# A list scheduler that orders a two-block kernel's engine work: measured operation times in its cost table in place of estimates

## The chip, the cores and the metric

The kernel runs on one core of a Trainium2 chip. Times are device microseconds (us) of one execution of the whole program on that core. PE is the matrix engine, DVE the vector engine, ACT the scalar engine, POOL the GpSimd engine and SP the engine whose queue issues most DMAs. Each engine takes its own instructions strictly in the order in which the program emits them, and waits on semaphores for what other engines have to deliver.

## What is computed

The input is x, 1024 tokens of 1024 numbers in float32. Two blocks run one after the other, and the result of the second is the output:

```python
def first_block(x, mem, ...):
    h = rms_norm(x, norm_mix);  proj = h @ w_in
    # 8 query heads over 2 key/value heads, a window of 128, plus a gated spatial unit
    attn = sliding_window_attention(q, k, v, attn_sinks)
    sg = spatial_gating(u, g, sgu_norm, sgu_w, sgu_b)
    x = x + concat(rms_norm(attn), rms_norm(sg)) @ w_out
    x = x + memory_cross_attention(rms_norm(x, norm_cross), mem_n, ...)
    x = x + hierarchical_moe(rms_norm(x, norm_ffn), ...)     # 4 groups x 8 experts, top 2 of a group
...
def second_block(x, c, w_mod, b_mod, ...):
    shift1, scale1, gate1, shift2, scale2, gate2 = split(silu(c) @ w_mod + b_mod, 6)
    h = rms_norm_2(x, g_norm1) * (1 + scale1) + shift1
    x_lru, z_lru, q, k, v = split(h @ w_in)
    y_lru = (rg_lru(conv(x_lru), forwards) + rg_lru(conv(x_lru), backwards)) * gelu(z_lru)
    y_att = diff_attention(q, k, v, ...)                     # 4 heads: softmax 1 - lam * softmax 2
    x = x + gate1 * (concat(y_lru, y_att) @ w_out)
    h2 = rms_norm_2(x, g_norm2) * (1 + scale2) + shift2
    x = x + gate2 * expert_choice_ffn(h2, ...)               # 16 experts, each takes its top 128 tokens
```

An expert of the first block is `(silu(xe @ w1) * (xe @ w3)) @ w2` with 512 hidden numbers; one of the second has 1024.

## The kernel before

**Tiles.** The tokens are eight tiles of 128. Every large product is taken to more than one pass of precision: a weight chunk of 128x1024 numbers (512 KB) comes by DMA into `wraw` (L369), ACT copies it to `wh` (L384) in the matrix engine's rounded format, and DVE, or POOL where the schedule picks it, takes the rest `wl = wraw - wh` (L389). The activations are split alike when they are transposed (`xT_h` by ACT at L247, `xT_l` by DVE at L249). Each 128x512 step then is three matmuls, `wh` by the high part (L339), `wl` by the high part (L340), `wh` by the low part (L341), and a chunk has two such steps, six matmuls. Where columns of a weight are to be scaled by a gain, POOL does it in `wraw` first (L379).

**Stages**, by the trace: the first block's mixers to 690 us, its routing to 745, 32 experts (the "first expert loop") to about 1365, the second block's projections and recurrence to 1675, differential attention to 1859, output product and the expert choice to 2045, and 16 experts (the "second expert loop") to 2600.

**An expert** (`expert1` in the first loop) gathers its rows (`xe`, a POOL DMA, L1507), transposes them (`p_t`), makes `p_a` and `p_b` from four chunks of w1 and four of w3, multiplies `hid = silu(p_a) * p_b` on DVE (L1536), transposes that (`p_ht`, L269; the copies of it to SBUF are `hidT`, on ACT L247 and DVE L249), makes two `p_y` from four chunks of w2, scales them on ACT (`y`, L1550) and adds them into the output by an indirect DMA that POOL issues (L1559). The second block starts after the last of these.

**Differential attention** runs for each of 32 pairs of head and token tile: scores `p_sc` on PE (L2108, L2109), bias and maximum on DVE (L2115), exponentials on ACT (L2098), the two softmaxes combined into `s` on DVE (L2145) or on ACT and POOL (L2148, L2150), four transposes `p_wt` (L312) copied to `wT` by ACT (L315) or DVE (L317), the product `p_o` (L2159), a norm (its root on POOL, L2166), `o` on DVE (L2170) and a transpose `p_ot` (L2175).

**The expert choice** (`top_part`) finds each expert's 128 largest of 512 tokens in one half of the tokens, and a second part does the other half: 16 rounds on DVE of eight maxima (L2307), a replacement (L2310) and their indices (L2312). `p_top` (L2338) transposes the result.

**What sets the order.** No order is written out. Every piece of work is a Python generator that yields, ahead of the instructions it emits, `S.op(engine, cost)`, `S.get(class)` for a buffer, or `S.wait(event)`. `Sched.run` (L100 on) keeps a clock for each engine; of all pieces that may run it takes the one with the earliest start, and among equal starts the one with the better priority. The clock moves on by the cost given, and what depends on the result may start `HOP` later. Where a piece names two engines (`wl` on DVE or POOL, `wT` on ACT or DVE), the one that would end first by these clocks is taken. So the costs set the order of each engine's instructions, the choice of engine, and which loads are issued first; the chip then runs each engine's list at its own pace. Buffers are counted by class (48 slots in all are shared by weights and activations).

## Time and profile before

| | us |
| --- | --- |
| median of 3 runs (2614.12 to 2623.0) | 2618.95 |
| the profiled execution | 2611.75 |
| its span on the core | 2609.7 |
| PE busy in the span | 2396.9 (92%) |
| DVE busy | 1964.9 (75%) |
| ACT busy | 1573.1 (60%) |
| POOL busy | 484.5 (19%) |

The profiled execution is 7.2 us under the median of the runs, and 2.05 us of it lie outside the span. Busy times count instructions in flight. The matmuls of one product overlap in the profile: one is listed with about 0.39 us and the next begins 0.23 us after it. An engine's idle time is listed with the instruction that it waited for, and this is what the rows below show.

### The profile page before, as it was taken

The numbers are of one execution on the slowest core, as the hardware profiler recorded it, in microseconds if no ns is written. First come the engines' busy times: TensorE is split into PE (matmuls) and PEld (weight loads), VectorE is DVE, ScalarE is ACT, GpSimd is POOL, SyncE is SP. The second block draws the span as 40 slices with busy tenths as digits, with TensorE's granted clock in tenths as the row PEclk, the third lists the DMA queues.
The fourth block names the chain that finished last, engine by engine and source line by source line (L and its number), as shares of the span: only waits on it lengthen the run. The fifth ranks groups of instructions, "written<-read, shape, count | busy, mean of one in ns | idle before, by whom it ended". The sixth has DMA issues, their size and how long they took to land. (4 is left out here: it accounts for less than half of the span.)

```text
span 2609.7 us, 34986 instructions
## 1 busy us (share of the span) xinstructions
PE 2396.9 (92%) x11984; PEld 1973.6 (76%) x11984; DVE 1964.9 (75%) x3179; ACT 1573.1 (60%) x2414; POOL 484.5 (19%) x383
## 2 busy tenths in 40 slices
PE   7999999999889899999987999999892999999998
PEld 6888887888667777777765777788682788877786
DVE  6568558555788888888876547599649799899997
ACT  5357225442357778777774558587422777677775
POOL 1021011100321224111112201034533000110010
PEclk9999999999989999999998999999996999999999
DMA  4433465224579999999994212753326899999997
GB/s 155 150 114 102 166 243 213 60 82 167 187 256 310 320 316 312 356 338 345 347 304 127 72 60 75 196 143 107 126 97 229 283 362 359 375 372 378 375 375 254
DMA packets 314581, 600.70 MB, mean 230 GB/s; under 512 B 33097, under 2 KB 64397, under 8 KB 314401
## 3 DMA queue, kind: packets, MB, share of 16 engines
q1 hardware_dynamic: 299936, 562.74, 61.6%
q0 software_dynamic: 14464, 35.71, 5.5%
q8 instruction: 95, 1.56, 0.2%
q14 instruction: 86, 0.70, 0.1%
HBM read 554.25 MB, written 60.87 MB: 236 GB/s over the span
## 5 line engine op out<-in xcount | busy, mean ns | idle before, releaser
L389 DVE TENSOR_TENSOR wl<-wraw,wh 128x1024 fp32r<-128x1024 f32 x829 | 992.9, 1241 | 128.9 <-ACT wh L384 118.4
L384 ACT ACTIVATE wh<-wraw 128x1024 fp32r<-128x1024 f32 x852 | 846.1, 1051 | 89.3 <-DMA wraw<-in_w_ck_dram 34.4
L260 POOL TENSOR_TENSOR rs_r<-rs_v,mhalf 128x1 f32<-128x1 f32 (+2 forms) x111 | 103.6, 935 | 788.0 <-DVE rs_v L257 787.8
L340 PE MATMUL p_b<-wl,xT_h 128*128 128x512 f32 x512 | 203.0, 396 | 9.1 <-DVE wl L389 9.1
L340 PE MATMUL p_a<-wl,xT_h 128*128 128x512 f32 x512 | 204.1, 399 | 5.7 <-DVE wl L389 5.4
L339 PE MATMUL p_b<-wh,xT_h 128*128 128x512 f32 x512 | 205.4, 401 | 1.6 <-ACT wh L384 1.6
L339 PE MATMUL p_a<-wh,xT_h 128*128 128x512 f32 x512 | 206.3, 403 | 0.0
L341 PE MATMUL p_a<-wh,xT_l 128*128 128x512 f32 x512 | 201.3, 393 | 0.2 <-DVE xT_l L249 0.2
L341 PE MATMUL p_b<-wh,xT_l 128*128 128x512 f32 x512 | 200.7, 392 | 0.0
L339 PE MATMUL p_g<-wh,aT_h 128*128 128x512 f32 x384 | 157.4, 410 | 0.0
L341 PE MATMUL p_g<-wh,aT_l 128*128 128x512 f32 x384 | 150.9, 393 | 0.0
L340 PE MATMUL p_g<-wl,aT_h 128*128 128x512 f32 x384 | 150.8, 393 | 0.0
L1559 POOL DMA_INDIRECT x_d<-y,tok x32 | 59.7, 1864 | 347.2 <-ACT y L1550 327.7
L340 PEld LDWEIGHTS p_a<-wl,xT_h 128*128 128x128 f32 x512 | 97.1, 190 | 35.3 <-DVE wl L389 17.1
L340 PEld LDWEIGHTS p_b<-wl,xT_h 128*128 128x128 f32 x512 | 96.7, 189 | 35.5 <-DVE wl L389 16.9
L2399 POOL DMA_INDIRECT out_dram<-y,tok x16 | 38.0, 2372 | 451.2 <-DVE y L2389 346.3
L247 ACT ACTIVATE xT_h<-p_t 128x512 fp32r<-128x512 f32 x96 | 56.7, 595 | 97.7 <-PE p_t L269 97.1
L339 PEld LDWEIGHTS p_b<-wh,xT_h 128*128 128x128 f32 x512 | 96.7, 189 | 21.0 <-ACT wh L384 1.9
L341 PEld LDWEIGHTS p_a<-wh,xT_l 128*128 128x128 f32 x512 | 96.8, 189 | 20.2 <-DVE xT_l L249 0.6
L339 PEld LDWEIGHTS p_a<-wh,xT_h 128*128 128x128 f32 x512 | 97.2, 190 | 19.0
L341 PEld LDWEIGHTS p_b<-wh,xT_l 128*128 128x128 f32 x512 | 96.4, 188 | 19.6
L340 PE MATMUL p_y<-wl,hidT 128*128 128x512 f32 x256 | 103.9, 406 | 4.6 <-DVE wl L389 4.3
(500 smaller groups left out, 5801.1 us busy)
## 6 DMA issues: line engine op xcount, KB each, us to landing
wraw<-in_w_dram SPq DMA_DIRECT2D x768, 512.0 KB, 9.2
mraw<-in_w_mod_dram SPq DMA_DIRECT2D x48, 512.0 KB, 5.2
x<-x_d SPq DMA_DIRECT2D x32, 512.0 KB, 4.2
wraw<-in_w_in_dram SPq DMA_DIRECT2D x28, 512.0 KB, 7.9
wraw<-in_w_out_dram SPq DMA_DIRECT2D x16, 512.0 KB, 3.5
hd<-kT_d SPq DMA_DIRECT2D x32, 256.0 KB, 5.5
x<-in_x_dram SPq DMA_DIRECT2D x8, 512.0 KB
xres<-in_x_dram SPq DMA_DIRECT2D x8, 512.0 KB
```

The costliest lines, as they stand in the source:

```text
L247: nc.scalar.activation(hi, src, AF.Copy)
L260: nc.gpsimd.tensor_tensor(r, v, self.mhalf[:, :w], op=OP.pow)
L339: nc.tensor.matmul(out, hh(k), wh, start=(k == 0), stop=False)
L340: nc.tensor.matmul(out, hh(k), wl, start=False, stop=False)
L341: nc.tensor.matmul(out, hl(k), wh, start=False, stop=(k == KK - 1))
L384: nc.scalar.activation(hi, raw, AF.Copy)
L389: (nc.vector if S.chosen == "DVE" else nc.gpsimd).tensor_tensor(lo, raw, f(hi), op=OP.subtract)
L1559: nc.gpsimd.indirect_dma_start(out=x_d, out_offset=bass.IndirectOffsetOnAxis(ap=k.tok[:, e:e + 1], axis=0), in_=y, in_offset=None, compute ...
L2399: nc.gpsimd.indirect_dma_start(out=out, out_offset=bass.IndirectOffsetOnAxis(ap=k.tok2[:, e:e + 1], axis=0), in_=y, in_offset=None, comput ...
```

## The change

Only numbers that the scheduler reads are changed; no instruction is added or taken away by hand, and no dependency. `HOP`, the distance from one operation's end to the start of what depends on it, goes from 0.12 to 0.2 us. The costs of an ACT, DVE and POOL operation on n numbers for each partition get other constants, a matmul of 512 columns goes from 0.216 to 0.227 us, the root in `rstd` (POOL) gets a higher cost, and the three operations of a round in `top_part` get constants of their own.

```diff
-    HOP = 0.12
+    HOP = 0.2
...
 def t_act(n, aps=0):
-    return 0.06 + n / 1200 + 0.093 * aps
+    return 0.13 + n / 1200 + 0.17 * aps
...
 def t_dve(n):
-    return 0.07 + n / 960
+    return 0.1 + n / 960
...
 def t_pool(n):
-    return 0.1 + n * 0.00225
+    return 0.2 + n * 0.0024
...
 def t_mm(n):
-    return max(0.107, n / 2400 + 0.003)
+    return max(0.109, n / 2400 + 0.0135)
...
-        yield S.op("POOL", 0.35 + 0.12 * w)
+        yield S.op("POOL", 0.5 + 0.16 * w)
...
-        yield S.op("DVE", t_dve(N))
+        yield S.op("DVE", 0.14 + N / 960)
         nc.vector.max(vi[:16, 0, s8], src)
         if r < 15:
-            e = yield S.op("DVE", t_dve(N))
+            e = yield S.op("DVE", 0.21 + N / 960)
             nc.vector.match_replace(dst, vi[:16, 0, s8], src, -1.0)
-        yield S.op("DVE", t_dve(N), after=[e - 0.3])
+        yield S.op("DVE", 0.2 + N / 960, after=[e - 0.3])
```

The instructions stay the same in number apart from the engine that takes some of them: of the 64 copies `wT`, ACT has 40 and DVE 24 before, 31 and 33 now; DVE makes 828 instead of 825 of the 128x1024 `wl`, POOL 20 instead of 23, besides one of 128x512. Everywhere the order moves. Three places follow, each before and after. In the rows "waits" names the engine or the DMA whose semaphore the instruction waits for.

PE in the first expert loop, around the transposes of `hid` of expert 12 (counted from 0), before:

```order
4252 L340 MATMUL p_a<-wl,xT_h 128x512
4253 L341 MATMUL p_a<-wh,xT_l 128x512
4254 L269 MATMUL p_t<-ident,xe 128x128 [waits DMASW3_49,PE_49]
4255 L269 MATMUL p_t<-ident,xe 128x128 x3
4256 L339 MATMUL p_a<-wh,xT_h 128x512 [waits Activation_49]
4257 L340 MATMUL p_a<-wl,xT_h 128x512 [waits DVE_49]
4258 L341 MATMUL p_a<-wh,xT_l 128x512
4259 L339 MATMUL p_a<-wh,xT_h 128x512
4260 L340 MATMUL p_a<-wl,xT_h 128x512
4261 L341 MATMUL p_a<-wh,xT_l 128x512
4262 L269 MATMUL p_ht<-ident,hid 128x128 [waits DVE_49]
4263 L269 MATMUL p_ht<-ident,hid 128x128 x3
```

The same place in the changed kernel, with the last steps of this expert's `p_b` and the first of the next expert's `p_a`:

```order
4212 L339 MATMUL p_b<-wh,xT_h 128x512
4213 L340 MATMUL p_b<-wl,xT_h 128x512
4214 L341 MATMUL p_b<-wh,xT_l 128x512
4215 L339 MATMUL p_b<-wh,xT_h 128x512
4216 L340 MATMUL p_b<-wl,xT_h 128x512
4217 L341 MATMUL p_b<-wh,xT_l 128x512
4218 L2008 MATMUL p_rel<-ident,rel_tab 4x32 [waits DMAHW7_49,PE_49]
4219 L269 MATMUL p_ht<-ident,hid 128x128 [waits DVE_49]
4220 L269 MATMUL p_ht<-ident,hid 128x128 x3
4221 L339 MATMUL p_a<-wh,xT_h 128x512 [waits PE_49,Activation_49]
```

Before, twelve matmuls of the next expert's `p_a` and four transposes `p_t` stand between the last of `p_b` (just ahead of these rows) and `p_ht`; now `p_ht` follows the last `p_b`, with one small transpose (`p_rel`) between.

DVE at the end of the first expert loop, from expert 30's `hid` to the first operation of the second block (L257), before:

```order
1367 L1536 TENSOR_TENSOR hid<-hid,p_b 128x512
1368 L389 TENSOR_TENSOR wl<-wraw,wh 128x1024 x2
1369 L249 TENSOR_TENSOR hidT<-p_ht,hidT 128x512
1370 L389 TENSOR_TENSOR wl<-wraw,wh 128x1024 x11
1371 L1536 TENSOR_TENSOR hid<-hid,p_b 128x512
1372 L389 TENSOR_TENSOR wl<-wraw,wh 128x1024 x2
1373 L249 TENSOR_TENSOR hidT<-p_ht,hidT 128x512
1374 L389 TENSOR_TENSOR wl<-wraw,wh 128x1024 x10
1375 L257 TENSOR_SCALAR rs_v<-ss 128x1
```

In the changed kernel:

```order
1357 L1536 TENSOR_TENSOR hid<-hid,p_b 128x512
1358 L249 TENSOR_TENSOR xT_l<-p_t,xT_h 128x512
1359 L389 TENSOR_TENSOR wl<-wraw,wh 128x1024
1360 L249 TENSOR_TENSOR hidT<-p_ht,hidT 128x512
1361 L389 TENSOR_TENSOR wl<-wraw,wh 128x1024 x10
1362 L1536 TENSOR_TENSOR hid<-hid,p_b 128x512
1363 L249 TENSOR_TENSOR hidT<-p_ht,hidT 128x512
1364 L389 TENSOR_TENSOR wl<-wraw,wh 128x1024 x5
1365 L257 TENSOR_SCALAR rs_v<-ss 128x1
```

Of the ten `wl` at the end of the first piece, the last five belong to the second block's first weights, `in_w_in`. Before, expert 31's `hid` (L1536, the second in either piece) is made ahead of them all and ahead of expert 31's own w2 chunks. Now it comes behind all four of those chunks and behind two of `in_w_in`; the other five, behind `hidT`, are of `in_w_in` too. On PE the whole of expert 31's `p_y`, 24 matmuls, stands behind its `p_ht` and its `hidT` in both kernels; before, 18 matmuls of expert 30's `p_y` lie between that `p_ht` and expert 31's first `p_y`, now none.

POOL in differential attention, at the second pair of scalings L379 of the output weights, before:

```order
206 L2150 TENSOR_TENSOR s_16959<-s_16959,s_16960 128x512
207 L2166 TENSOR_TENSOR r_17291<-v_17290,mhalf 128x1
208 L2150 TENSOR_TENSOR s_16965<-s_16965,s_16966 128x512 x2
209 L2166 TENSOR_TENSOR r_17364<-v_17363,mhalf 128x1
210 L2150 TENSOR_TENSOR s_16981<-s_16981,s_16982 128x512
211 L379 TENSOR_TENSOR wraw<-wraw,grow 128x1024 x2
212 L2166 TENSOR_TENSOR r_17451<-v_17450,mhalf 128x1
```

And in the changed kernel:

```order
203 L2166 TENSOR_TENSOR r_17292<-v_17291,mhalf 128x1
204 L2150 TENSOR_TENSOR s_16986<-s_16986,s_16987 128x512
205 L2166 TENSOR_TENSOR r_17353<-v_17352,mhalf 128x1
206 L2150 TENSOR_TENSOR s_16986<-s_16986,s_16987 128x512
207 L379 TENSOR_TENSOR wraw<-wraw,grow 128x1024
208 L2150 TENSOR_TENSOR s_17024<-s_17024,s_17025 128x512
209 L2166 TENSOR_TENSOR r_17454<-v_17453,mhalf 128x1
210 L379 TENSOR_TENSOR wraw<-wraw,grow 128x1024
```

Two scalings in a row have become two single ones with an addition of `s` (L2150) and a root (L2166) between.

## Rows read from the trace of the kernel before

**Rows 1.** windows by stage: times, length, each engine's busy us, clock, DMA share, GB/s

```profile
745.00:1050.00 305.00, 281.53 (x1287) 228.41 (x1286) 262.04 (x286) 232.53 (x281) 78.64 (x72) 0.98 0.92 316
1050.00:1350.00 300.00, 286.23 (x1295) 225.10 (x1294) 251.72 (x244) 231.19 (x273) 49.80 (x28) 1.00 1.00 347
1675.00:1859.00 184.00, 166.40 (x1092) 145.27 (x1091) 166.79 (x512) 141.87 (x309) 74.12 (x69) 0.94 0.50 147
2045.00:2600.00 555.00, 547.91 (x2491) 443.39 (x2489) 503.09 (x492) 403.31 (x458) 57.88 (x29) 1.00 1.01 360
```

**Rows 2.** waits of PE, 745 to 1050: line, releaser, us in total, times, longest

```profile
PE p_ht L269 <- DVE hid L1536: 10.2, 7, 2.7
```

**Rows 3.** waits of PE in the second half (1050 to 1350)

```profile
PE p_b L340 <- DVE wl L389: 9.1, 12, 0.8
PE p_ht L269 <- DVE hid L1536: 0.8, 1, 0.8
```

**Rows 4.** waits of SP's DMA queue in the same stretch

```profile
SPq L369 <- DMA wraw<-in_w_dram: 80.5, 110, 2.4
```

**Rows 5.** timeline of PE: start, length, operation, [idle before, its releaser]

```profile
966.16 0.66 PE L269 MATMUL p_ht<-ident,hid 128*128 128x128 f32 x4 [1.53 <-DVE hid L1536]
...
1331.39 0.66 PE L269 MATMUL p_ht<-ident,hid 128*128 128x128 f32 x4 [0.78 <-DVE hid L1536]
...
1348.45 0.39 PE L341 MATMUL p_b<-wh,xT_l 128*128 128x512 f32 x1
1348.67 0.39 PE L339 MATMUL p_b<-wh,xT_h 128*128 128x512 f32 x1
```

**Rows 6.** timeline of POOL at the end of the first expert loop

```profile
1365.32 1.69 POOL L1559 DMA_INDIRECT x_d<-y,tok  x1 [3.22 <-issue]
```

**Rows 7.** timeline of DVE there

```profile
1361.88 1.22 DVE L389 TENSOR_TENSOR wl<-wraw,wh 128x1024 fp32r<-128x1024 f32 x1 [0.41 <-ACT wh L384]
```

**Rows 8.** timeline of ACT there

```profile
1361.75 0.69 ACT L1550 ACTIVATE y<-p_y,gate_tab 128x512 f32<-128x512 f32 x1
```

**Rows 9.** timeline of DVE in the routing of the first expert stage

```profile
699.30 2.18 DVE L1289 SCALAR_TENSOR_TENSOR r_w<-lg,r_w,desc 128x4 f32<-128x4 f32 x1
...
706.58 0.23 DVE L1289 SCALAR_TENSOR_TENSOR r_w<-r_w,desc 128x8 f32<-128x8 f32 x1
```

**Rows 10.** timeline of POOL there

```profile
693.40 12.66 POOL L389 TENSOR_TENSOR wl<-wraw,wh 128x1024 fp32r<-128x1024 f32 x5 [0.21 <-ACT wh L384]
```

**Rows 11.** waits of PE in the differential attention (1675 to 1859)

```profile
PE p_ot L2175 <- DVE o L2170: 5.6, 8, 2.8
PE p_wt L312 <- DVE s L2145: 4.1, 3, 1.8
```

**Rows 12.** timeline of POOL in the differential attention

```profile
1790.20 4.72 POOL L379 TENSOR_TENSOR wraw<-wraw,grow 128x1024 f32<-128x1024 f32 x2
...
1825.57 5.17 POOL L379 TENSOR_TENSOR wraw<-wraw,grow 128x1024 f32<-128x1024 f32 x2
```

**Rows 13.** timeline of DVE in the differential attention

```profile
1793.20 2.27 DVE L2145 SCALAR_TENSOR_TENSOR s<-s,c,s 128x512 f32<-128x512 f32 x1
...
1797.20 0.74 DVE L2145 SCALAR_TENSOR_TENSOR s<-s,c,s 128x512 f32<-128x512 f32 x1
```

**Rows 14.** groups by line in that stretch: count, busy us, mean ns, idle before

```profile
L317 DVE COPY wT<-p_wt 128x512 f32<-128x512 f32 x24 | 16.0, 682 | 1.9 <-PE p_wt L312 1.9
```

**Rows 15.** timeline of DVE around the second part's first round of eight maxima

```profile
1986.53 0.22 DVE L2285 TENSOR_REDUCE r2s<-r 128x4 f32<-128x64 f32 x1 [0.38 <-ACT r L2283]
...
1988.95 0.68 DVE L2307 MAX8 topv<-aff 16x8 f32<-16x512 f32 x1 [1.73 <-ACT aff L2298]
```

**Rows 16.** waits of PE after the differential attention (1859 to 2045)

```profile
PE p_top L2338 <- DVE topv L2332: 33.9, 1, 33.9
```

**Rows 17.** the windows view inside the second expert loop

```profile
2100.00:2150.00 50.00, 50.00 (x236) 41.38 (x235) 46.96 (x48) 39.12 (x46) 4.65 (x3) 1.00 1.04 366
2400.00:2450.00 50.00, 48.82 (x218) 38.73 (x218) 46.09 (x45) 36.66 (x41) 6.15 (x4) 1.00 1.05 379
```

## The prediction

> **What bounds the kernel now.** I read the table of windows by stage first, then the waits of PE in each stage, then the timelines where a wait is long. PE is busy for 281.53 of 305 us and 286.23 of 300 us in the two halves of the first expert loop, for 547.91 of 555 us in the second loop, and for 166.40 of 184 us in differential attention [rows 1]. So PE's own list is the bound in most of the program, and an order can win only what PE now waits, or lose what it would wait anew. The stages differ in what stands behind PE. In the second half of the first loop the DMA engines are full (share 1.00, 347 GB/s), PE's waits are small ones for `wl` [rows 3], and SP, which issues the loads, itself waits for earlier loads for 80.5 us [rows 4]: there the loads set the pace. In the first half the share is 0.92 and PE's largest wait is for `hid` ahead of `p_ht`, 10.2 us in 7 waits [rows 2]. In attention PE waits for DVE, above all for `o` and `s` [rows 11], and DVE is busy for 166.79 of 184 us. In the expert choice one wait of 33.9 us is a chain on DVE that no order shortens [rows 16].
>
> **The change part by part.** No work is added, so each term is a wait that comes or goes. The sum is made against the profiled execution, 2611.75 us, and carried over to the median, 2618.95, as a difference.
>
> *First expert loop, first half.* `p_ht` needs `hid`, which DVE makes after the last matmul of `p_b`. What hides this is whatever PE has between the two. I counted, in both orders, the experts with less than half a microsecond of matmuls there. Of experts 0 to 15 they are 6 before and 10 now, expert 12 among the new ones. An uncovered one costs an idle PE of 0.78 to 1.53 us [rows 5]. Four more cost 4 x 0.78 to 4 x 1.53, so 3 to 6 us. Some of the newly covered ones, the first two above all, give 1 to 3 us back. I take +3, with bounds of 0 and +6.
>
> *Second half.* Of experts 16 to 31, 2 are uncovered before and 15 now, 13 more: 13 x 0.78 to 13 x 1.53 is 10 to 20 us of new waits on PE. But here PE waits for the loads anyway, 9.1 us for `wl` in `p_b` alone [rows 3], and a wait for `hid` only takes their place as long as loads arrive no later. SP's 80.5 us [rows 4] say that the loads don't hang on PE. I take 0, and +8 as the upper bound.
>
> *The end of the loop.* This is the largest single term. The second block begins with the last scatter, which starts at 1365.32 [rows 6], after the last `y` (1361.75 plus 0.69) [rows 8] and after the scatter before it. In the new order DVE makes expert 31's `hid` only behind the `wl` of two chunks of the next block's weights. In the trace the second of these starts at 1361.88 and takes 1.22, so it ends at 1363.1 [rows 7]. If the loads keep their pace, `hid`, `p_ht` and `hidT` follow: `hid` and the first `hidT` some 0.7 each, by the DVE and ACT steps on 512 numbers (0.682 and 0.69) [rows 8, 14], and `p_ht` 0.66 [rows 5], so the first of the 24 matmuls of `p_y` starts near 1365.2. They go at one in 0.22 to 0.23 us [rows 5], 5.4 us in all, and `y` adds 0.7: the last scatter could start near 1371.3 to 1372. That is 6.0 to 6.7 later, and nothing hides it, since PE has nothing else until the next block's first tile is back. I take +6.5. The bounds are 0, if the loads run ahead by that much, and +10, if the new waits have made them late as well.
>
> *First routing.* Five `wl` in a row on POOL fill 12.66 us [rows 10], and in this stretch DVE's tiny operations stretch: one on 4 numbers takes 2.18 us, the same line on 8 numbers later 0.23 [rows 9]. Each further `wl` there costs the routing chain up to a POOL `wl`, 12.66 / 5 = 2.5 us. The new order has four in this place instead of five, about -2, and takes the first product of a routing tile about 1 later on PE. I take -1, bounds -3 and +2.
>
> *Expert choice.* DVE sits idle for 0.38 and 1.73 us ahead of the second part's first round [rows 15]; the new order puts the last rounds of the first part there. -2, bounds -2.1 and +1.4 (an affinity product stands later on PE).
>
> *Attention.* PE idles for 17.6 of the 184 us, and the clock of 0.94 costs a few more [rows 1]. The new order starts the scores further ahead of `p_wt` (on average 12 us of PE work between them instead of 10, as I count the matmuls there at 0.23 each), which should take a part of the 5.6 and 4.1 us waited for `o` and `s` [rows 11]. The scalings L379 run in pairs of 4.72 and 5.17 us [rows 12], and inside such a pair one `s` on DVE takes 2.27 instead of 0.74 us [rows 13]; the second pair is split. Against this DVE gets 9 more copies `wT`, 9 x 0.682 = 6.1 us [rows 14], and six operations of the recurrence's last piece, some 7 us by an estimate from the 0.68 of a 512-number copy, of which they do up to two, with 184 - 166.79 = 17.2 us free. I take -3. All of PE's idle time cannot go; two thirds are -12 and the lower bound. The upper is +6: of 13 us more DVE work, half would then fall on the path.
>
> By the Trainium skill ("SBUF — State Buffer", section "Who interferes with whom"), a DVE operation with two SBUF inputs and a GpSimd operation that reads SBUF lock each other out, and the second to issue blocks for the whole of the first. The stretched `s` in the trace agrees (2.27 against 0.74). By that rule a split pair blocks for as long as two singles, so the split itself would bring nothing, and the attention's term would be about -1 instead of -3 and the sum 2 us higher.
>
> *Second expert loop.* Where the order keeps chunks ready ahead of PE, PE is busy for 50.00 of 50 us and starts 236 matmuls; where it takes them as they come, 48.82 and 218 [rows 17]. The new order keeps several chunks in hand for about 140 us longer. 1.18 of 50 us is 2.4%, and of 140 us that is 3.3; by the matmuls (8% fewer) it would be 11, though not all stretches are as scarce. But the DMA share is 1.04 and 1.05 in the two rows [rows 17], so that the loads may set the end all the same. I take -3, bounds -8 and 0.
>
> *The rest* (the first mixers, the recurrence, the tail) moves without a wait that I can name: 0, within 3 either way.
>
> The sum is 3 + 0 + 6.5 - 1 - 2 - 3 - 3 + 0 = +0.5: 2612.3 for the profiled execution, 2619.5 for the median.
>
> **The rivals.** *Offsets* (the forecast): what the earlier scores and spare chunks win, the first loop's end gives back. About 2619.5; it includes the case in which the order matters little because loads and DVE chains hold the time. For it speaks that no term exceeds a few microseconds and the signs are mixed.
>
> *The deeper schedule wins.* With dependences priced longer, work starts further ahead in attention and both routings. Two thirds of the attention's wait go (-12), the choice and routing give -5, the second loop -6, and the loop's end costs 6.5 as above, the first half nothing: -16.5, so 2602.5. For it speaks PE's idle time in attention, for which DVE is named each time [rows 11]; against it DVE's small reserve.
>
> *The uncovered `p_ht` is paid in full (slower).* The place is PE in the first loop, behind each last `p_b`. If PE and not the loads sets the pace in the second half, 13 more waits of 0.78 to 1.53 us, 15 on the middle value, come on top of the sum: 0.5 + 15 = +15.5, so 2634.5. It decides from the point at which these waits exceed what PE now waits for `wl` there, 9.1 us in `p_b` [rows 3]. Against it speaks the full DMA; for it, that a DMA which waits for buffers that PE frees later gets slower with PE.
>
> *The costs change nothing,* that is, the order is the same: excluded, the order moves on all engines.
>
> **How the numbers follow.** A measurement of this kernel can tell about 0.3%, 7.9 us, from no change. The forecast's case, its own range 2611 to 2627, has 0.42. The deeper schedule has 0.31 and the paid `p_ht` 0.27; these are also the chances of faster and slower. The range has to reach into both: 2601 to the low side, near the second case's time, and 2638 to the high, a little past the third's; outside lie together about 0.2. Predicted: 2619.5.
>
> **What would show it.** In the changed profile the waits `p_ht` for `hid` grow by a few in the first half and to 15 in the second, with the waits for `wl` in `p_b` shrinking there; the last scatter of the loop starts 6 us later than the length of the loop explains; PE's waits for `o` and `s` in attention fall by a few microseconds and DVE is above 0.93 busy there; in the expert choice the idle time ahead of the second part's first round is gone. The prediction is wrong if SP waits more for PE's releases than for loads in the second half (then 2634), if the last loads of the first loop arrive 6 us earlier than their place in it, or if attention shortens by 10 us.

## The result

The changed kernel takes 2643.43 us in the median (2640.3 to 2644.0, 4 runs), the kernel before 2619.68 beside it (2614.12 to 2623.0): a ratio of 1.0096, interval 1.0084 to 1.0109, or 24 us slower. The forecast of 2619.5 is missed, and so is its range, by 5 us. The profiled execution of the changed kernel took 2644.0 us (span 2642.3), about its median; that of before took 2611.75, 8 below its own. Differences between the two profiles therefore add up to 32 us, 9 more than the medians differ by.

The first table cuts the spans at the first or last matmul of the lines that open and close a stage on PE; the first 19 to 20 us, before the first product, are left out. The third row is one of the kernels tried below.

| us | first block's mixers and routing | first expert loop | recurrence, projections | attention | expert choice | second loop, tail |
|---|---|---|---|---|---|---|
| before | 713.4 | 647.8 | 294.5 | 181.4 | 165.9 | 587.5 |
| after | 725.3 | 672.4 | 279.4 | 191.4 | 165.3 | 588.2 |
| `hop_mixed_lat` | 709.3 | 653.0 | 287.0 | 175.9 | 169.2 | 583.8 |

Three stages lose (+12, +25, +10), one wins (-15), two stand. How far a stage length can be trusted is told by the kernels below that have the changed kernel's order in it: the mixers come out at 723.0 to 727.6 us, the first loop at 672.2 to 674.6, attention at 188.1 to 191.4. The border between recurrence and attention moves with the order, since 8.4 us of DVE's recurrence work now lie behind it; the two stages together go from 475.9 to 470.8 us.

The windows view of the changed kernel, by the same stages as [rows 1] (times, length, busy us of PE, PEld, DVE, ACT and POOL with counts, clock, DMA share, GB/s):

```profile
756.00:1061.00 305.00, 273.82 (x1226) 220.62 (x1225) 252.81 (x277) 224.79 (x269) 71.52 (x68) 0.96 0.91 311
1061.00:1361.00 300.00, 275.49 (x1291) 224.42 (x1289) 249.05 (x243) 230.82 (x279) 51.82 (x29) 1.00 0.99 347
1697.00:1891.00 194.00, 169.80 (x1092) 144.85 (x1090) 181.12 (x528) 141.10 (x300) 71.97 (x68) 0.94 0.48 141
2077.00:2632.00 555.00, 544.52 (x2492) 445.30 (x2491) 504.98 (x493) 416.70 (x459) 68.29 (x29) 1.00 1.01 360
```

PE is less busy in both halves of the first loop than in [rows 1] (273.82 for 281.53, 275.49 for 286.23), though the DMA share in the second half is the same (0.99 for 1.00). In attention PE's list is the same 1092 matmuls, but DVE is busy for 181.12 of 194 us instead of 166.79 of 184.

PE's waits for `hid` in the first loop (line, releaser, us in total, times, longest), in the first of these windows and in the second, where they are all that PE waits for:

```profile
PE p_ht L269 <- DVE hid L1536: 13.3, 10, 3.3
...
PE p_ht L269 <- DVE hid L1536: 20.2, 14, 1.5
```

and those of SP's DMA queue in the second, the two largest:

```profile
SPq L369 <- DMA wraw<-in_w_dram: 99.3, 133, 1.6
SPq L369 <- PE p_a L340: 22.8, 13, 4.5
```

Against [rows 3] the 9.1 us for `wl` in `p_b` are gone and the waits for `hid` stand in their place, 14 instead of 1. SP waits even longer for earlier loads than in [rows 4] (99.3 for 80.5). So far, in the second half, this is what the prediction said, and by its rule it should cost nothing. The loop became 25 us longer all the same, and the experiments had to find out where.

### The profile page after: what moved, and what is told of

Same layout as the page of the kernel before. It is cut to its first block, busy times and chain, and to the rows that moved or that the text cites. A ratio compares the mean times of both kernels' runs of the same rounds, so it can differ in the third digit from the quotient of the medians.

```text
span 2642.3 us, 34838 instructions
## 1 busy us (share of the span) xinstructions
PE 2396.4 (91%) x11984; PEld 1982.8 (75%) x11984; DVE 1975.3 (75%) x3197; ACT 1575.1 (60%) x2399; POOL 493.1 (19%) x377
## 5 line engine op out<-in xcount | busy, mean ns | idle before, releaser
L384 ACT ACTIVATE wh<-wraw 128x1024 fp32r<-128x1024 f32 x852 | 858.2, 1052 | 118.0 <-DMA wraw<-in_w_dram 48.6
L260 POOL TENSOR_TENSOR rs_r<-rs_v,mhalf 128x1 f32<-128x1 f32 (+2 forms) x111 | 111.0, 1002 | 752.5 <-DVE rs_v L257 705.5
L2399 POOL DMA_INDIRECT out_dram<-y,tok x16 | 51.0, 3185 | 415.0 <-DVE y L2389 336.8
L340 PE MATMUL p_y<-wl,hT_h 128*128 128x512 f32 x256 | 100.7, 394 | 6.1 <-DVE wl L389 6.1
```

Source lines behind the costliest of these rows:

```text
L260: nc.gpsimd.tensor_tensor(r, v, self.mhalf[:, :w], op=OP.pow)
L340: nc.tensor.matmul(out, hh(k), wl, start=False, stop=False)
L384: nc.scalar.activation(hi, raw, AF.Copy)
L2399: nc.gpsimd.indirect_dma_start(out=out, out_offset=bass.IndirectOffsetOnAxis(ap=k.tok2[:, e:e + 1], axis=0), in_=y, in_offset=None, comput ...
```

## The experiments

The planner's `lat` is the time by which it believes a result to be readable after the operation's end. Raising it on one operation changes nothing but the order, and with it the engine where the schedule has a choice. Each ratio is to the kernel before in the same comparison (2616.5 to 2618.6 us). Each expectation sets a theory A against a theory B.

### The first loop: `p_ht`, or the chunks ahead of the last `hid`

`hid_lat` gives the planner a later `hid` in the first block's experts (uncovered `p_ht`, those with less than half a microsecond of matmuls ahead of them since the last of `p_b`, fall from 25 to 9 of 32); `gate_w_in` holds the conversion of the first `in_w_in` chunks back until expert 31's `hid` is made, by an event `k.h31`.

```
 hid_lat, cut from the edit (L1535)
-    yield S.op("DVE", t_dve(512))
+    yield S.op("DVE", t_dve(512), lat=1.2)
 gate_w_in, cut from the edit (L1536, L2438; the event is made at L1599)
+    e == 31 and S.set(k.h31)
+    [setattr(y, 'gate', k.h31) for y in w[:LW]]
```

> The changed kernel, with one more number: the scheduler is told that hid (DVE, L1536) can be read 1.2 us later than its cost says, so that it places p_ht later on PE. In the first expert loop's first half, experts with under half a microsecond of matmuls between p_b and p_ht go from 10 to 5, in the second half from 15 to 4. Theory A (the uncovered p_ht, with the low clock behind it, is what made the first half of that loop longer): PE's waits of p_ht for hid in the first 300 us of the loop fall from 13.3 us to 5 to 7, this half is 6 to 10 us shorter, the second half unchanged, the whole 6 to 10 us faster than the changed kernel (about 2635). Theory B (the first half is longer because weights and routing come later, and a wait for hid only replaces one for wl): the p_ht waits fall all the same, waits for wl come in their place, the whole within 3 us of the changed kernel.

> The changed kernel, in which the splits of the next block's first weights (in_w_in) may not be placed ahead of expert 31's hid. On DVE two wl and on ACT two wh fewer stand ahead of it, and so it can be made 2.3 us earlier if these were what it waited for. Theory A (the prediction's: hid waits behind the wl of in_w_in): the end of the first loop is 4 to 7 us earlier, the whole 3 to 7 us faster than the changed kernel. Theory B (hid is ready when PE has done p_b, and PE is late for another reason, the low clock and the order on ACT): within 2 us of the changed kernel.

`hid_lat`: 2630.56 us, ratio 1.0055 (1.0039 to 1.0072); the loop falls from 672.4 to 659.4. That is more than theory A told, and it lies in another place: 7.5 us come back up to the 17th `hid`, 7.4 from there to the 32nd, and in the first 300 us PE still waits 15.6 us for `hid`, in 5 waits. `gate_w_in`: 2644.88, 1.0103 (1.0081 to 1.0125), theory B; the loop stays at 672.3. DVE's timeline at the end of the loop in `gate_w_in` (start, length, operation, [idle before, its releaser]) tells why:

```profile
1361.16 1.23 DVE L1719 SCALAR_TENSOR_TENSOR gmod<-mscale,gmod 128x1024 f32<-128x1024 f32 x1 [10.26 <-DMA mscale<-mod_d]
1362.30 9.16 DVE L389 TENSOR_TENSOR wl<-wraw,wh 128x1024 fp32r<-128x1024 f32 x8
...
1389.20 0.69 DVE L1536 TENSOR_TENSOR hid<-hid,p_b 128x512 f32<-128x512 f32 x1 [2.92 <-PE p_b L341]
```

With the chunks out of the way, DVE stands idle for 2.92 us ahead of the last `hid`, waiting for PE's `p_b`. The last expert's `hid` was not held by DVE's queue; PE itself comes late. The same view of the changed kernel says so too:

```profile
1359.04 1.23 DVE L1719 SCALAR_TENSOR_TENSOR gmod<-mscale,gmod 128x1024 f32<-128x1024 f32 x1 [9.53 <-DMA mscale<-mod_d]
1360.18 9.16 DVE L389 TENSOR_TENSOR wl<-wraw,wh 128x1024 fp32r<-128x1024 f32 x8
...
1388.63 0.69 DVE L1536 TENSOR_TENSOR hid<-hid,p_b 128x512 f32<-128x512 f32 x1 [0.65 <-PE p_b L341]
```

Its first row is a wait that nobody had looked for. DVE takes its instructions in order, and `gmod` (L1719), a small step that the next block needs much later, stands in front of eight `wl` while its operand is still on its way. The DMA queue of SP shows when that operand was asked for:

```profile
1348.53 0.33 SPq L237 DMA_DIRECT2D mscale<-mod_d  x1
```

The load needs some 10.5 us, from 1348.53 to 1359.04, in a stretch with a DMA share near 1; the planner's figure for it is about 3.5. Before, the load took longer, 12.9 us from its issue at 1315.12, but the step stood later in DVE's list, at 1329.07, and did not wait.

### How far PE runs behind the loads

The loads end at nearly the same time in both kernels: the issue of the experts' last one starts 613.7 us after the loop's start before and 616.2 now, and ends at 614.8 and 616.7. So the 25 us must lie between the loads and PE. The second table gives, for some experts in their order, the time from the issue of the expert's last `w3` chunk to its `hid`, from the start times in the traces (experts and their `hid` are counted from 1 to 32 from here on); "end" is the time from the issue of the last load to the end of the loop.

| us, expert no. | 5 | 9 | 13 | 17 | 21 | 25 | 30 | 31 | 32 | end | loop |
|---|---|---|---|---|---|---|---|---|---|---|---|
| before | 45.7 | 36.3 | 40.2 | 23.1 | 16.0 | 12.6 | 11.5 | 10.1 | 10.7 | 34.1 | 647.8 |
| after | 48.0 | 38.8 | 44.3 | 38.7 | 32.1 | 31.1 | 28.7 | 35.9 | 32.2 | 56.2 | 672.4 |
| `hid_lat` | 47.1 | 37.3 | 46.7 | 31.6 | 27.6 | 27.9 | 26.6 | 25.6 | 22.5 | 48.3 | 659.4 |
| `hid_mscale_late` | 51.8 | 38.0 | 40.0 | 26.6 | 26.1 | 27.4 | 26.9 | 27.3 | 20.8 | 46.0 | 657.2 |
| `no_mm` | 47.2 | 39.3 | 40.2 | 28.8 | 24.0 | 12.0 | 12.7 | 8.4 | 13.1 | 36.8 | 656.6 |
| `hop_mixed_lat` | 44.2 | 40.6 | 46.8 | 33.1 | 30.4 | 23.5 | 14.6 | 9.7 | 11.5 | 39.5 | 653.0 |

Before, PE catches up with the loads to about 11 us and from then on waits for `wl`. In the changed kernel it runs 29 to 39 us behind through the whole second half and is 32.2 behind at the last expert. While loads arrive, such arrears cost nothing; when they end, PE still has them to work off. From the last load's issue to the loop's end it takes 56.2 us instead of 34.1; these 22.1 and the 2.5 by which that issue starts later are the 24.6 us.

The traces also tell how the arrears come about. Up to expert 17 the loads keep the same pace in both kernels. But between the 5th and the 17th `hid` PE takes 13.8 us longer, and its waits of `p_ht` for `hid` are 14.1 us in 10 there instead of 5.7 in 5: the windows by time above, 13.3 against 10.2, hide this. From the 17th `hid` to the 30th PE takes 249.8 us, of which it waits 17.1, all for `hid`, while the loads advance by 259.8. Without these waits, by an estimate, its 38.7 us of arrears would have shrunk to 11.6, where the kernel before stands at 11.5. About half of each wait is DVE's order. Expert 25's last `p_b` in the changed kernel ends at 1224.60, but `hid` stands behind a `wl` on DVE and starts 0.79 us later (two rows of DVE's timeline, then one of PE's):

```profile
1223.11 2.36 DVE L389 TENSOR_TENSOR wl<-wraw,wh 128x1024 fp32r<-128x1024 f32 x2 [0.73 <-ACT wh L384]
1225.39 0.68 DVE L1536 TENSOR_TENSOR hid<-hid,p_b 128x512 f32<-128x512 f32 x1
...
1226.12 0.66 PE L269 MATMUL p_ht<-ident,hid 128*128 128x128 f32 x4 [1.52 <-DVE hid L1536]
```

Experts 19 to 30 all have this delay of 0.79 us.

Two runs take this apart. `mscale_late` makes the planner believe in a later landing of the `mscale` loads alone (one in the loop, one in attention); `hid_mscale_late` does that and leaves only 4 `p_ht` uncovered.

```
 cut from the edits: both (end of L1717)
+    yield S.op("LATE", 0.0, lat=10.0)
 hid_mscale_late (L1535)
+    yield S.op("DVE", t_dve(512), lat=1.6)
```

> The changed kernel, with one edit: the planner is told that the last load of mscale before the end of the first loop lands 10 us later than it thinks, so that VectorE's gmod behind it (L1719) moves behind twelve more of the loads' conversions (wl). The uncovered p_ht stay at 10 and 15. Theory A (the 11.8 us that the loop lost between expert 16's hid and expert 31's are VectorE's 9.5 us wait in order for that load, with the conversions queued behind it): the wait goes, that stretch comes back from 297.2 to 286-289 us, and the run to 2631-2635 us, about 10 below the changed kernel. Theory B (the stretch is long for the 15 uncovered p_ht, which hid_lat also removed): the stretch stays at 295-298 us and the run within 3 us of the changed kernel's 2643.4.

> The changed kernel with two edits: the planner believes that hid lands 1.6 us later (4 p_ht of 32 stay uncovered in place of 25), and that the last mscale load lands 10 us later. What is compared is the time from the issue of an expert's last w3 chunk to its hid: it falls from 23.1 us at expert 17 to 10.7 at expert 32 in the kernel before, from 38.7 to 28.7 (expert 30) and 32.2 in the changed one, and the experts' last load is issued 614.8 and 616.7 us after the loop begins in the two. Theory A (TensorE runs behind the loads through the second half, cannot catch up while a p_ht wait of 1.4 us stands in each expert, and the arrears are paid when the loads end): the time falls to 12-18 us at expert 32, the loop is 648-657 us long and the run 2615-2626 us. Theory B (hid_lat's 659 us is what the changed order allows; its arrears of 22.5 us come from elsewhere): the time at expert 32 stays at 20-25 us, the loop at 657-662 and the run at 2626-2633 us.

`mscale_late`: 2639.11 us, 1.0094 (1.0065 to 1.0123), neither theory's figure. DVE's step has no idle time before it any more:

```profile
1365.90 1.22 DVE L1719 SCALAR_TENSOR_TENSOR gmod<-mscale,gmod 128x1024 f32<-128x1024 f32 x1
```

and the arrears at experts 31 and 32 are 29.3 and 25.6 instead of 35.9 and 32.2. The three other kernels with the changed loop have 30.6 and 30.7 at expert 32, so the wait was 5 to 7 us of the arrears. But in this run the experts' loads also ended 4.9 us later (621.6), and the loop is only 3 us shorter: as a gain in time the wait is not shown.

`hid_mscale_late`: 2628.58, 1.0035 (1.0024 to 1.0047), the loop 657.2. That was theory B's case: the arrears stay near 26 and end at 20.8. But the run does not take the waits away, and so it does not show whether they are the whole reason why PE does not catch up. The few that are left are long in this order, since `hid` starts up to 3.9 us after the end of its `p_b`, behind `wl` on DVE. PE's waits in it, from 1075 to 1340:

```profile
PE p_ht L269 <- DVE hid L1536: 13.6, 5, 3.8
PE p_y L339 <- ACT hidT L247: 3.0, 3, 1.5
PE p_y L341 <- DVE hidT L249: 2.4, 4, 0.6
```

Before, PE's idle time in the second half is nearly all waiting for chunks [rows 3], the mark of an engine that has caught up. Here it is mostly the chain from `p_b` over `hid` and `hidT` to `p_y`, and its waits for chunks (`wl`) come to 1.9 us. From the 17th `hid` to the 30th PE waits 17.0 us in all, as long as in the changed kernel. In `hid_lat` it is only 8.9, but there 1101 matmuls stand in this stretch instead of 1085, and the granted clock is 0.98. So an order that places more of other experts' matmuls ahead of `hid` shows up as arrears too.

The reverse experiment gives the planner of the kernel before a later `hid` (`lat=1.8` at L1535; uncovered `p_ht` 6 and 1 become none).

> The kernel before, told that hid can be read 1.8 us later than its cost says. By the order no p_ht is uncovered any more (0 and 0, least cover 0.9 us). Theory A (each uncovered p_ht of the first half costs PE 0.8 to 1.5 us and some of the low clock): PE's waits of p_ht for hid fall from 11 us to under 3, and the first loop is 5 to 10 us shorter, the whole 5 to 10 us faster than the kernel before (about 2611). Theory B (the loop is held by its loads): waits for wl or for the loads come in their place, within 3 us of the kernel before.

2616.56 us, 1.0001 (0.9993 to 1.001), theory B: the first half still waits 12.2 us for `hid`, in 7 waits of up to 4.7, and with arrears of 14.4 us at the end against 10.7 there was nothing to win.

### The first mixers and attention

In the mixers, the place of the loss shows as waits of PE between 220 and 300 us:

```profile
PE p_t L288 <- DVE nm L672: 7.3, 2, 3.9
PE p_t L288 <- DVE mixed L729: 1.3, 1, 1.3
```

PE does not wait there for either of them before. And the granted clock falls behind them, in the windows view of the changed kernel:

```profile
230.00:241.00 11.00, 7.13 (x63) 6.95 (x63) 9.43 (x32) 4.95 (x16) 2.20 (x2) 1.00 0.62 223
241.00:251.00 10.00, 9.14 (x46) 8.77 (x45) 7.28 (x18) 5.80 (x16) 1.65 (x1) 0.51 0.31 97
251.00:261.00 10.00, 6.31 (x52) 5.89 (x50) 8.86 (x26) 7.20 (x19) 1.46 (x1) 0.97 0.51 167
261.00:265.00 4.00, 3.35 (x17) 3.38 (x17) 3.49 (x10) 2.01 (x8) 0.00 (x0) 0.60 0.02 4
...
275.00:282.00 7.00, 7.00 (x28) 6.23 (x27) 3.69 (x8) 1.57 (x5) 0.00 (x0) 0.53 0.27 68
```

PE waits 3.87 us before 240.3 and then runs for 10 us at 0.51 (1.2 GHz), where its 9.14 busy us would have been some 4.7 at full clock by an estimate (9.14 x 0.51). The second wait, 3.44 us, is followed by 4 us at 0.60; the third stretch, 7 us at 0.53, comes behind waits of 1.38 and 1.34 us. The kernel before has low stretches there too, about 10 us in all (at 249 and 263) against 20 now. From the first `p_o` to the last PE takes 11.7 us longer, with 8.3 us more idle time: that is nearly all that the stage loses. `mixed_lat` gives the planner a later `mixed`; `wT_act` moves copies `wT` in attention from DVE to ACT (DVE keeps 14 of its 33); `three_fixes` is these two and `hid_lat` at once.

```
 mixed_lat, cut from the edit (L728)
-    yield S.op("DVE", t_dve(512))
+    yield S.op("DVE", t_dve(512), lat=3.0)
 wT_act, cut from the edit (L313)
-            yield S.op(("ACT", "DVE"), (t_act(n), t_dve(n)))
+            yield S.op(("ACT", "DVE"), (t_act(n) - 0.3 if name == "p_wt" else t_act(n), t_dve(n)))
```

> The changed kernel, told that the normed attention output (DVE, L729) can be read 3 us later than its cost says, so that the transposes p_t of it stand later on PE: the least PE work between p_o and p_t goes from 0.9 us (two tiles) to 2.8. Theory A (the 12 us lost near 230 to 290 us are these two waits and the low clock that follows them): 8 to 12 us come back there, PE's waits of p_t for nm (L672) and the low clock vanish, the whole is 8 to 12 us faster than the changed kernel (about 2633). Theory B (DVE is simply full in this stretch): the waits go to another transposition or to p_o, less than 3 us come back.

> The changed kernel, in which the choice of an engine for the 64 copies wT favours ACT by 0.3 us: ACT makes 50 and DVE 14 instead of 31 and 33. Theory A (DVE is the bound of differential attention, it is busy there for 181 of 194 us): 19 copies of 0.68 us leave DVE, 13 us, the stage is 6 to 10 us shorter than in the changed kernel, and PE's waits for o (L2170) and mx (L2115) fall. Theory B (the chains of the attention tiles are what PE waits for, and ACT takes its place): within 3 us of the changed kernel, PE waits for wT on ACT (L315) instead.

> The changed kernel with the three corrections that took time back each for itself: hid later by 1.2 us (12.9 us back), the normed attention output later by 3 us (10.5), the copies wT on ACT (5.6). Theory A (the loss is a sum of separate waits, each at its own place): they add up, 29 us back, 2612 to 2618, no slower than the kernel before. Theory B (one wait takes the place of another): at most 18 us back, 2625 or more.

`mixed_lat`: 2632.9, 1.0064 (1.0039 to 1.0089); the mixers 718.1 us, so 7 of the 12 come back. PE's waits for `nm` are gone, as theory A told, but two for `mixed` (L719) of 5.8 us stand in their place. `wT_act`: 2637.79, 1.0071 (1.0047 to 1.0094); attention 184.9 instead of 191.4, and 3 to 4 us below the other kernels with this order (188.1 to 189.0). The intervals of these two runs overlap with the changed kernel's, so their gain is read from the stage. `three_fixes`: 2617.12, 0.9992 (0.998 to 1.0004), theory A's case: the three together take the change's loss away. No stage is quite back, though (718.5, 660.1, 184.5 us, still 5, 12 and 3 above the kernel before); the recurrence's 13 us pay for most of that.

PE's waits in attention, in the changed kernel, beside [rows 11]:

```profile
PE p_ot L2175 <- DVE o L2170: 9.8, 9, 2.1
PE p_sc L2108 <- DVE mx L2115: 4.8, 4, 2.2
PE p_wt L312 <- DVE s L2145: 4.8, 6, 1.4
```

All are for DVE, and all have grown (`o` from 5.6, `s` from 4.1, `mx` from 1.5). DVE's groups in the stretch from 1697 to 1891 name its new work:

```profile
L317 DVE COPY wT<-p_wt 128x512 f32<-128x512 f32 x33 | 22.0, 682 | 1.6 <-PE p_wt L312 1.1
L1920 DVE TENSOR_TENSOR_SCAN l_a<-l_a,l_g 128x1024 f32<-128x1024 f32 x1 | 2.3, 2287 | 0.0
L1911 DVE SCALAR_TENSOR_TENSOR l_g<-l_a,l_g 128x1024 f32<-128x1024 f32 x1 | 1.2, 1226 | 18.9 <-ACT l_a L1909 18.9
```

Nine more copies (22.0 for 16.0 us, [rows 14]) and six operations of the recurrence, 8.4 us in all, 2.29 for the scan and 1.22 for the others. In `wT_act` DVE is busy for 169.69 of 185 us.

### The parts of the change

Each of the following is the kernel before with a part of the new numbers, or the changed kernel without one.

```
 only_hop: HOP = 0.2 (was 0.12)
 only_mm:  return max(0.109, n / 2400 + 0.0135)
 only_act_dve: t_act, t_dve and the costs of the expert choice
 no_act_dve:   HOP, t_mm and the POOL costs
 no_mm:        all but t_mm
 hop_mixed_lat: only_hop and mixed_lat's edit
 hop_mixed_wT:  hop_mixed_lat and wT_act's edit
```

> The kernel before with the new matmul cost alone. By the order: experts with an uncovered p_ht 7 and 8 in the two halves of the first loop (before 6 and 1, changed kernel 10 and 15); least PE work between p_o and p_t in the late tiles of the first attention 2.8 us (before 2.6, changed kernel 0.9); DVE takes 22 of the copies wT (24, 33). Theory A (these three counts carry the loss): within 5 us of the kernel before, with each of the three stages within 3 us of it. Theory B (the loss comes from the changed pace of PE against the loads in the plan, which the matmul cost alone sets): the first loop is 8 us or more longer than before.

> The kernel before with the new HOP alone. By the order: uncovered p_ht 10 and 9, least PE work between p_o and p_t 0.4 us (one tile), DVE takes 22 of the copies wT. Theory A (the counts carry the loss): the first loop's first half 5 to 9 us longer than before, the first mixers 2 to 5 us longer, differential attention not longer; the whole 6 to 14 us slower than before. Theory B: the same as the kernel before within 4 us.

> The kernel before with the new ACT and DVE costs alone (with those of the eight maxima). By the order: uncovered p_ht 10 and 7, least PE work between p_o and p_t 0.9 us in two tiles, DVE takes 35 of the copies wT. Theory A (the counts carry the loss): the first loop's first half 5 to 9 us longer than before, the first mixers 6 to 12, differential attention 7 to 12 as in the changed kernel: the whole 18 to 28 us slower than before, as slow as the changed kernel or nearly. Theory B (it takes the change of all costs together): at most half of that, within 12 us.

> The kernel before with the new HOP, the new matmul cost and the new POOL costs, but the old ACT and DVE costs (and those of the eight maxima). By the order: uncovered p_ht 5 and 4, least PE work between p_o and p_t in the late tiles 2.3 us, DVE takes 29 of the copies wT. Theory A (the higher ACT and DVE costs, together with HOP, make the plan's chains so long that PE has used up its independent work when it gets to them): the first mixers within 5 us of before, the first loop within 5, the recurrence 7 us shorter as with HOP alone: 2605 to 2614. Theory B (HOP and the matmul cost do it between them): 2625 or more.

> The changed kernel without the new matmul cost. By the order: uncovered p_ht 6 and 5 (changed kernel 10 and 15), least PE work between p_o and p_t 1.0 us in one tile (0.9 in two), DVE takes 29 of the copies wT (33). Theory A (the matmul cost alone does nothing, but with the others it takes PE's spare work from behind p_b; the loop's loss goes with the count): the first loop 12 us or more shorter than in the changed kernel, the whole 2620 to 2630. Theory B (the loop's loss comes from the ACT and DVE costs alone): the loop within 5 us of the changed kernel.

> The kernel before with the new HOP and the normed attention output later by 3 us. HOP alone measured 2610 with the first mixers 6 us longer than before, in which PE waits 6.7 us for p_t of mixed; least PE work between p_o and p_t goes from 0.4 to 3.2 us. Theory A: these 6 us come back, 2603 to 2607. Theory B (as with the changed kernel, less than half comes back, since DVE is full there): 2607 to 2611.

> The kernel before, with the changed HOP (0.2), the later landing of mixed (lat=3.0) and the wT copies favoured onto ScalarE (5 of 64 left on VectorE). hop_mixed_lat, without the last, gave 2599.3 us with an attention of 175.9 us. Theory A (VectorE bounds attention, as wT_act showed from a busier VectorE): attention falls by 3-6 us and the run to 2593-2597 us. Theory B (with 22 copies on VectorE it no longer binds, and ScalarE's longer queue costs as much): attention 174-178 us and the run 2597-2603 us.

| | us | ratio to before | mixers, routing | first loop | recurrence | attention |
|---|---|---|---|---|---|---|
| `only_mm` | 2615.25 | 0.9993 (0.998 to 1.0006) | 720.9 | 649.7 | 293.6 | 181.9 |
| `only_hop` | 2610.05 | 0.9971 (0.996 to 0.9981) | 719.5 | 651.4 | 287.7 | 175.9 |
| `only_act_dve` | 2631.03 | 1.0052 (1.0033 to 1.007) | 734.4 | 655.1 | 286.0 | 182.0 |
| `no_act_dve` | 2616.63 | 1.0001 (0.9991 to 1.0011) | 713.8 | 653.7 | 293.0 | 177.5 |
| `no_mm` | 2624.69 | 1.0031 (1.0019 to 1.0044) | 717.7 | 656.6 | 285.5 | 186.1 |
| `hop_mixed_lat` | 2599.34 | 0.993 (0.9916 to 0.9944) | 709.3 | 653.0 | 287.0 | 175.9 |
| `hop_mixed_wT` | 2597.74 | 0.9932 (0.9906 to 0.9957) | 708.1 | 652.1 | 287.1 | 175.1 |

The longer `HOP` alone, one of the change's numbers, makes the kernel faster, which neither of its theories told. The new DVE and ACT times alone make it slower, most of all in the mixers and routing, by more than theory B and less than theory A told. `only_mm` and `no_mm` keep to their theory A in the whole, `no_act_dve` falls between its two, and `hop_mixed_lat` is faster than either. Yet the counts do not foretell the stages: by the order `only_mm` has 2.8 us of cover in the mixers, no less than before, and its mixers and routing are 7.5 us longer. The loop's arrears need the parts together: in each of the first five kernels of this table PE catches up (10.5 to 13.1 us at the last expert). All five have 27.5 to 33.1 us at expert 17, where the changed kernel has 38.7, and PE waits 8.8 to 12.0 us from there to the 30th `hid`, not 17.1. `no_mm` shows it in PE's waits from 1060 to 1330, where those for `wl` are back:

```profile
PE p_ht L269 <- DVE hid L1536: 4.7, 5, 2.0
PE p_y L340 <- DVE wl L389: 4.0, 9, 1.0
PE p_a L340 <- DVE wl L389: 2.3, 4, 1.1
```

`only_hop` still waits in the mixers, and `hop_mixed_lat` removes that: its clock from 240 to 285 is full throughout.

```profile
240.00:285.00 45.00, 42.55 (x265) 36.92 (x266) 35.40 (x94) 23.88 (x74) 0.62 (x2) 1.00 0.60 212
```

It beats both kernels, by 0.7% the one before. In the loop it waits for `hid` too, 9.9 us in 8 waits between the 17th `hid` and the 30th, and it catches up all the same. Taking more `wT` from DVE adds nothing that can be told (2597.74 for 2599.34), theory B's case: with the 22 copies of this order on DVE attention is no longer bound by them.

## Why the prediction was wrong, step by step

**First loop, first half (+3): right as a wait, wrong as a cost.** From the loop's start to the 17th `hid` PE takes 346.9 us instead of 330.1, 16.8 more, where the upper bound was +6. The waits of `p_ht` for `hid` grow by 8.4 us between the 5th `hid` and the 17th, more than the 3 to 6 us that four more uncovered ones were to cost; the rest is other waits and a clock of 0.96 for 0.98, which the term left out. At expert 17 PE is 15.6 us further behind the loads than before; why the order has the other waits stays open.

**Second half (0): the replacement came as told, and was still paid.** 14 waits (against 1 before, where the prediction counted 2 uncovered), the `wl` waits gone, the DMA full, the last load 1.9 us later. Yet from the 17th `hid` to the 32nd PE takes 296.1 us instead of 286.9, 9.2 more. The step that failed is "a wait for `hid` only takes their place as long as loads arrive no later". PE's waits for `wl` were the sign that it had caught up, 11 us behind the loads. Waits that come while it is still behind do not replace those; they keep it behind, and the arrears fall due at the loop's end. The two halves need each other: `only_hop` waits 9.9 us for `hid` from expert 17 to 30 with 33.1 us of arrears and still catches up, the changed kernel with 38.7 and 17.1 does not. The rival "the uncovered `p_ht` is paid in full" thus came nearest (2634.5), and its condition, that SP waits more for PE than for loads, was the wrong test: SP's 99.3 us for loads stayed the longest. Nor did the 80.5 us say that the loads do not hang on PE: over all lines SP waited 76 us for PE before, and 66 now. That the waits are the cause is told by the sums in the trace; no run takes them away and leaves the rest of the order alone. Of the 21.5 us between 32.2 and 10.7, 5 to 7 are the wait for `mscale` by the arrears, which no step of the prediction had. Why the planner's order has these waits only with all the new numbers stays open.

**The end of the loop (+6.5): wrong.** The last `hid` waits 0.65 us for PE and not for DVE's queue, holding back the chunks gave nothing, and from that `hid` to the loop's end it takes 29.4 us instead of 30.8. The working took the order of DVE's list for the time at which things happen; PE's arrival was left as it was before.

**Attention (-3): wrong in sign.** In the order the scores do stand further ahead, but the waits for `o` and `s` grew. The additional DVE work was priced about rightly (13 us told; 6.0 and 8.4 measured), its effect was not: DVE had 17 us free over the whole stage, but not where its answers were due, and 7 to 10 of 14 us fell on the path, above the upper bound of +6. The part of it that the Trainium skill had spoken on ("SBUF — State Buffer", section "Who interferes with whom") is small: the scalings L379 that the change splits take 2.40 and 2.35 us one by one, and `s` (L2145) has a mean of 846 instead of 903 ns, under 2 us over the stage. So the trace agrees that a split of the pair brings little.

**First routing (-1), expert choice (-2), second loop (-3): not seen.** The choice is 0.6 us shorter, its wait `p_top` 35.3 instead of 33.9 us [rows 16]. The second loop is 0.7 longer, PE 544.52 us busy for 547.91. From the first `p_pos` (L1329) to the loop's first `p_a` it takes 125.7 us instead of 124.1, so no gain is seen; the last mixer tiles lie in the same stretch.

**The rest (0, within 3): two misses that cancel.** The mixers cost 12 us (`mixed_lat` gives 7 back), and the recurrence won 15. There PE's waits for `qks` shrink by 6.3 us, and the clock over these stretches is 0.98 instead of 0.96. In the kernel before, between 1380 and 1675:

```profile
PE p_qt L269 <- DVE qks L249: 8.7, 4, 2.9
```

and in the changed one, between 1418 and 1697:

```profile
PE p_qt L269 <- DVE qks L249: 2.4, 3, 1.3
```

These two stages make up 27 of the 62 us that moved, and they had been given nothing since no wait was named there before. But a stage without waits can lose by a new order: the mixers had cover of 2.6 us between `p_o` and `p_t` of `mixed`, counted in the order, and the new order left 0.9. This could have been counted like the `p_ht` were and would have warned, though `only_mm` shows that the count gives no figure. That the two come to -3 together, within the term's bounds, is luck. The sum went wrong in the first loop (24.6 us for 9.5) and in attention (7 to 10 for -3).

## What to carry to other kernels

Where loads set the pace, compare how far the compute engine runs behind them, expert by expert, before calling its waits free: waits for loads mean that it has caught up, any other wait is a debt that falls due when the loads end, unless the engine has time to work it off. Compare waits from one expert to the same expert, not in windows of equal time. Truer costs in a list scheduler need not give a better order: here lengthening the believed latency at two places (the hop, and one result on PE's path) won 0.7% where the whole table of measured times lost 1%. Count the cover of each cross-engine dependence in every stage, the quiet ones too.

## What the runs showed of the hardware

A broadcast load of one row, `mscale`, took 10.5 us from issue to landing beside a full DMA queue, and 12.9 in the kernel before. DVE, which takes its instructions in order, passed a wait of 9.53 us for it on to all that stood behind, here eight conversions of 1.2 us. In the mixers a wait of PE of 3.87 us was followed by 10 us at a granted clock of 0.51 and one of 3.44 us by 4 us at 0.60, so that by an estimate from the busy times the clock cost another 4.5 and 1.3 us. The length of a single wait does not tell: 7 us at 0.53 followed waits of 1.38 and 1.34 us there, while 14 waits of up to 1.5 us in the loop's second half left the clock at 1.00.
